# A hybrid attention and retention layer on one core: paired projections traced product by product, retention blocks in thirds, three small operations on other engines

## The chip, the cores and the metric

The kernel runs on one core of one Trainium2 chip. The metric is device microseconds of one execution; the value of a kernel is the median of several runs. The core has TensorE (PE, matmuls and their weight loads), VectorE (DVE), ScalarE (ACT), GpSimd (POOL) and SyncE (SP), each with an instruction queue of its own that is worked off in order. SP and POOL also issue the DMAs of this kernel.

## The reference

One layer for a prompt of 1024 tokens and a sample group of 8 x 4 tokens (1056 columns in all), model width 1024. One input projection `w_in` gives the heads of two branches and three gates; windowed attention and chunkwise retention run side by side, each is projected and they are merged by gates; then `w_o` and a convolutional FFN.

```python
h = rms_norm(x, g_pre_mix) @ w_in
q_a, k_a, v_a, q_r, k_r, v_r, gate_r, gm_a, gm_r = jnp.split(h, split_points(), axis=-1)
o_a = banded_window_attn(q_a, k_a, v_a, pos, sinks)      # window 128, 8 heads, 2 kv heads
...
# retention, 4 heads, chunks of 128, key 128, value 256:
scores = jnp.einsum('bihd,bjhd->bhij', q, k) * dmask[None]
inner = jnp.einsum('bhij,bjhe->bihe', scores, v)
cross = jnp.einsum('bihd,bhde->bihe', q, s0) * q_decay[None, :, :, None]
s_new = jnp.exp(log_g * L)[None, :, None, None] * s0 + jnp.einsum('bjhd,bjhe->bhde', k * k_decay[None, :, :, None], v)
...
y_a = o_a @ w_a_proj
y_r = (jax.nn.silu(gate_r) * o_r) @ w_r_proj
mixed = (jax.nn.sigmoid(gm_a) * y_a + jax.nn.sigmoid(gm_r) * y_r) @ w_o
x = x + rms_norm(mixed, g_post_mix)
x = x + rms_norm(conv_ffn(rms_norm(x, g_pre_ffn)), g_post_ffn)
```

## The kernel before

Every fp32 product is made of three matmuls (`mm3`, lines 256 to 258): each operand is split into a high and a low part (`split`: the high part is an ACT copy, L229, the low part a subtraction, L224 on DVE or L226 on POOL), and high x high, high x low and low x high are summed in PSUM. Besides, the large projections are done with seven products instead of eight (`A11, A12, A22, S1` to `S4`), from sums of weight blocks and of activation columns. One product of the pair stage is 4 x 3 = 12 matmuls of 264 columns.

The stages follow each other: normalisation and the first projections, attention, the attention projection (`w_a`, tile ps_a) with sums of activations on DVE, the **pair stage**, the retention projection (`w_r`, tile ps_m and ps_t; here called the z stage), `w_o`, and the FFN.

*Attention.* `attn_pair` treats two of the four head groups in one block of 128 queries, 16 calls in all: scores, a softmax over them (`comb`, with the sum in `den`), four ACT multiplications by 1/den (L686), four transposes (L689), a split into `ph`, for 14 calls two products `pc` of `ph` with a triangle (L695), and the matmuls with the values (L702), whose two halves are added in `pvt` (L706). The sample group's attention (L745 to L755) follows.

*Pair stage.* Sixteen pairs of 128-column groups of `w_in` are projected, each in two halves of the columns (`in_pair`, a generator that yields after each half): four pairs for q and k of the four retention heads, four for the retention gate, eight for the merge gates. A half uses three PSUM banks q0, q1, q2 (tile ps_q, one buffer each). In the order A11, S1, S2, A12, S3, A22, S4, S2 needs a copy of A11's bank in bank 1 (L876); results leave by ACT copies (L884) or DVE additions (L887). `w_split` makes the high and low parts of the weights, three ahead when a pair begins. Work that follows a half (`post`: rope of q and k by a shuffle and products on DVE and POOL, gates on ACT, stores) is held in PEND until `flush`, after a later S2.

Beside the pairs run the retention of the sample group (`sample(h)`, between whole pairs) and that of the prompt (`head(h)`, eight blocks each). A block takes scores and a transpose of k into a ps_a tile (L1045, L1046), masks and splits them (s, sT), scales k (kt), splits v (vt), multiplies into ps_b, adds q (qs) times the state, updates the state from ps_a (L1066), normalises the output (`finish`, with rs on POOL, L283), transposes it (`turn`, L929) and multiplies it by the gate into z (L1081). PSUM holds three ps_a and two ps_b banks beside the three of ps_q.

*What sets the order.* The program is traced in Python; the framework schedules it on a simulated timeline, so an engine's order follows the traced order only roughly. `BLK` sets how many halves of pairs are traced by each retention block: 20 halves over the 32 blocks. Tile pools hold the buffers: a new tile waits until the buffer that it takes over has been read. Weight loads and gate loads go through SP's queue (`ld`), stores, and the loads of qk and v for the retention, through POOL's (`st`).

*z stage.* When a quarter of the result is complete, `merge` multiplies it by one gate and adds the other branch, two DVE operations of 128x528 (L1155, L1156), 16 times. The z operands are loaded on POOL's queue (L1105) in a fixed order.

Of the kernel before, what the change touches and what calls it, by code (L numbers as in the profile page):

```python
# [18 lines left out]
P = 128  # L19
# [3 lines left out]
NB = 8  # L23
# [82 lines left out]
BLK = 10  # L106
# [15 lines left out]
def trunk(ctx, tc, I, O):  # L122
# [539 lines left out]
    def attn_pair(jp, blk):  # L662
# [22 lines left out]
        for h in range(4):  # L685
            S.mul(comb[:, h, :P], comb[:, h, :P], den[:, h:h + 1])  # L686
# [5 lines left out]
        if blk:  # L692
            pc = AT("pc", (P, 2, 4, P), F32R, bufs=2)
            for s in range(2):
                V.tensor_tensor(out=pc[:, s], in0=f32(ph[:, s]), in1=tri.broadcast_to([P, 4, P]), op=mult)  # L695
# [69 lines left out]
    ps_stack.close()  # L765
    pq = ppool("pq", 1, ps_stack)
    pa = ppool("pa", 3, ps_stack)
# [91 lines left out]
    FILL = [5, 8, 6, 9, 7, 10, 11, 12, 13, 14, 15]  # L859
    NEXT = dict(zip([0, 1, 2, 3, 4] + FILL, [1, 2, 3, 4] + FILL + [None]))  # L860
    PW, PEND = [in_ahead(0)], []

    def in_pair(n):

        ws, post, ops = PW[0], pairs[n][2], {}
        for j in range(2):
            o = TT("pair")
            c11, c12, c21, c22 = (o[:, HW * i:HW * i + HW] for i in range(4))
            bk = [psum(pq, "q%d" % b)[:, :HW] for b in range(3)]
            for p in (A11, S1, S2, A12, S3, A22, S4):  # L870
                t = ops[p] = next(ws) if j == 0 else ops[p]
                ps = bk[{A11: 0, A12: 0, S2: 1, S3: 1, A22: 1, S1: 2, S4: 2}[p]]
                if p == S2:
                    if n == j == 0:
                        TE.matmul(ps, t[:, 0], xop(ex1, p, j, 0)[0], start=True, stop=True)
                    S.copy(out=ps, in_=bk[0])  # L876
                for k in range(4):
                    xh, xl = xop(ex1, p, j, k)
                    mm3(ps, t[:, k], t[:, 4 + k], xh, xl, p in (A11, S1) and k == 0, k == 3,
                        skip_group_check=p not in (A11, S1))  # L880
                if p == S2:
                    flush()
                if p in (A12, S1, S2, A22):
                    S.copy(out={A12: c11, S1: c22, S2: c12, A22: c21}[p], in_=ps)  # L884
                elif p != A11:
                    c = c22 if p == S3 else c12
                    V.tensor_tensor(out=c, in0=ps, in1=c, op=add)  # L887
# [741 lines left out]
```

## Time and profile before

| | us |
|---|---|
| runs | 1716.36, 1713.27, 1716.02; median 1716.02 |
| profiled execution, own time | 1712.92 |
| its span, first to last instruction | 1711.1 |
| start, normalisation | 0 to 50 |
| attention and projections beside it | 50 to 200 |
| end of attention, sample attention | 200 to 252 |
| attention projection | 252 to 299.6 |
| pair stage: sample retention, then the prompt's blocks (first score at 458.6), then pairs alone (from about 700) | 299.6 to 750.6 |
| z stage | 750.6 to 850 |
| `w_o` | 850 to 950 |
| FFN | 950 to 1700 |

How to read it: the windows give, for a stretch of the span, how long each engine was busy and how many instructions it ran. The waits name what released an engine that stood idle. The groups give count and duration for a kind of instruction. A line such as L224 is that of a helper and covers many uses, so the tile's name says which.

### The profile page before, as it was taken

The page shows a single profiled execution, that of the slowest core. Times are in us where ns is not written, and L with a number is a line of the kernel's source. Part 1 is how long each engine was busy: PE and PEld are TensorE (multiplying, and loading weights), DVE is VectorE, ACT ScalarE, POOL GpSimd, SP SyncE. Part 2 cuts the span into 40 slices and gives each one's busy share as a digit, 9 for nine tenths or more (in the row PEclk, how much of TensorE's full clock was granted, in tenths as well). Part 3 has the DMA queues.
Part 4 walks back from the last instruction along what each step waited for, and adds up shares of the span by engine and source line. Part 5 has one row for each costly group of instructions (what it writes and reads, how often), then busy time and mean ns, then how long its engine had stood idle before and what let it go on. Part 6 is the DMA issues. An engine that isn't in the chain of part 4 may idle for free.

```text
span 1711.1 us, 32973 instructions
## 1 busy us (share of the span) xinstructions
PE 1647.4 (96%) x12642; PEld 1600.9 (94%) x12642; DVE 1267.5 (74%) x2283; ACT 891.3 (52%) x2006; POOL 434.6 (25%) x658
## 2 busy tenths in 40 slices
PE   8999989898898999999999999999999999999997
PEld 7999979888887999999878999999999999999997
DVE  7787647799577777557956889888888888445576
ACT  6577634344565665454532555555555556433343
POOL 4211100365344443210111222212212223111101
PEclk9999989999998999999999999999999999999999
DMA  7212313345657776587732244444444447866654
GB/s 195 68 54 64 94 45 114 121 139 164 213 180 230 237 253 198 163 251 219 241 127 74 74 131 146 144 151 151 146 157 151 158 145 239 247 181 199 208 178 152
DMA packets 265871, 273.92 MB, mean 160 GB/s; under 512 B 22784, under 2 KB 225824, under 8 KB 265697
## 3 DMA queue, kind: packets, MB, share of 16 engines
q1 hardware_dynamic: 230673, 151.05, 30.4%
q0 software_dynamic: 35040, 120.77, 20.3%
q8 instruction: 99, 1.62, 0.4%
q14 instruction: 59, 0.48, 0.1%
HBM read 184.24 MB, written 87.49 MB: 159 GB/s over the span
## 4 chain that ended last, share of the span: by engine, by line
PE 59%; DMA 7%; DVE 5%; issue 3%; ACT 1%; POOL 1%; SPq 0%; DVEq 0%; POOLq 0%; ACTq 0%
PE ps_m L258 9%; PE ps_m L256 9%; PE ps_m L257 9%; PE ps_t L257 7%; PE ps_t L256 7%; PE ps_t L258 7%; PE ps_q L256 2%; PE ps_q L257 2%; PE ps_q L258 2%; DMA zt<-in_w_r_proj 1%; DMA w_raw<-in_w_in 1%; DMA zt<-in_w_down 1%; DMA w_raw<-r_d 1%; DMA vt<-v_d 1%; DVE zt L224 1%
## 5 line engine op out<-in xcount | busy, mean ns | idle before, releaser
L224 DVE SCALAR_TENSOR_TENSOR w_lo<-w_raw,w_hi 128x1024 fp32r<-128x1024 f32 x83 | 101.2, 1222 | 70.2 <-ACT w_hi L229 66.4
L256 PE MATMUL ps_t<-xh,w_hi 128*128 128x264 f32 (+2 forms) x524 | 149.2, 285 | 0.0
L257 PE MATMUL ps_t<-xl,w_hi 128*128 128x264 f32 (+2 forms) x524 | 148.7, 284 | 0.0
L256 PE MATMUL ps_m<-xh,w_hi 128*128 128x264 f32 x512 | 146.2, 286 | 2.4 <-ACT Gr L1163 0.9
L258 PE MATMUL ps_t<-xh,w_lo 128*128 128x264 f32 (+2 forms) x524 | 148.0, 283 | 0.0
L258 PE MATMUL ps_m<-xh,w_lo 128*128 128x264 f32 x512 | 145.6, 285 | 1.2 <-DVE w_lo L224 1.2
L257 PE MATMUL ps_m<-xl,w_hi 128*128 128x264 f32 x512 | 145.5, 284 | 0.0
L256 PE MATMUL ps_q<-ex,w 128*128 128x264 f32 x384 | 113.5, 295 | 13.2 <-ACT ps_q L876 8.8
L224 DVE SCALAR_TENSOR_TENSOR w<-w_raw,w 128x512 fp32r<-128x512 f32 x152 | 104.0, 684 | 29.5 <-ACT w L330 28.1
L1379 DVE SCALAR_TENSOR_TENSOR c_out<-u_ext,fconst,c_out 128x1024 f32<-128x1024 f32 x96 | 121.9, 1280 | 2.6 <-ACT c_out L1375 0.4
L229 ACT CAST w_hi<-w_raw 128x1024 fp32r<-128x1024 f32 x62 | 65.2, 1052 | 107.6 <-PE ps_t L257 74.5
L257 PE MATMUL ps_q<-ex,w 128*128 128x264 f32 x384 | 110.8, 289 | 0.0
L258 PE MATMUL ps_q<-ex,w 128*128 128x264 f32 x384 | 110.7, 288 | 0.0
L256 PE MATMUL ps_q<-xh,w 128*128 128x264 f32 x384 | 109.0, 288 | 0.6 <-DVE pair L887 0.6
L257 PE MATMUL ps_q<-xl,w 128*128 128x264 f32 x384 | 109.5, 287 | 0.0
L258 PE MATMUL ps_q<-xh,w 128*128 128x264 f32 x384 | 109.1, 287 | 0.0
L330 ACT CAST w<-w_raw 128x512 fp32r<-128x512 f32 x152 | 94.4, 622 | 27.3 <-PE ps_q L258 23.2
L256 PEld LDWEIGHTS ps_m<-xh,w_hi 128*128 128x128 f32 x512 | 96.3, 188 | 3.3 <-ACT Gr L1163 1.1
L258 PEld LDWEIGHTS ps_t<-xh,w_lo 128*128 128x128 f32 x524 | 98.8, 189 | 0.0
L256 PEld LDWEIGHTS ps_t<-xh,w_hi 128*128 128x128 f32 x524 | 98.6, 188 | 0.1
L257 PEld LDWEIGHTS ps_t<-xl,w_hi 128*128 128x128 f32 x524 | 98.7, 188 | 0.0
L258 PEld LDWEIGHTS ps_m<-xh,w_lo 128*128 128x128 f32 x512 | 96.4, 188 | 1.7 <-DVE w_lo L224 1.6
(465 smaller groups left out, 6264.2 us busy)
## 6 DMA issues: line engine op xcount, KB each, us to landing
w_raw<-in_w_up SPq DMA_DIRECT2D x48, 512.0 KB, 4.5
w_raw<-in_w_in SPq DMA_DIRECT2D x42, 512.0 KB, 5.3
w_raw<-s_d SPq DMA_DIRECT2D x60, 256.0 KB, 3.6
t_d<-t POOLq DMA_DIRECT2D x24, 528.0 KB, 4.0
t<-t_d POOLq DMA_DIRECT2D x24, 528.0 KB, 5.2
t<-in_w_down SPq DMA_DIRECT2D x40, 256.0 KB, 4.8
s_d<-t POOLq DMA_DIRECT2D x20, 512.0 KB, 3.6
w_raw<-in_w_down SPq DMA_DIRECT2D x36, 256.0 KB, 6.7
```

The costliest lines, as they stand in the source:

```text
L224: pinned(V.scalar_tensor_tensor(out=out, in0=in0, scalar=1.0, in1=in1, op0=mult, op1=op))
L229: pinned(S.copy(out=hi, in_=src))
L256: TE.matmul(ps, wh, xh, start=start, stop=False, **kw)
L257: TE.matmul(ps, wh, xl, start=False, stop=False, **kw)
L258: TE.matmul(ps, wl, xh, start=False, stop=stop, **kw)
L330: S.copy(out=t[:, 0:4], in_=src)
L1379: V.scalar_tensor_tensor(out=c[:, NS:], in0=u[:, g, NU + t:NU + t + SEQ], scalar=sc[t], in1=c[:, NS:], op0=mult, op1=add)
```

## The change

It rewrites the pair stage and moves three small kinds of work. In the pair stage:

- The pairs become one stream that yields after each product (`stream`, `adv(n)` takes n products). The order of products is A11, S1, A22 of the half before, S2, A12, S4, S3. A11's bank is copied into bank 1 right after A11. Bank 1 has two buffers, so ps_q uses four PSUM banks, and ps_a two instead of three. The weights of the next pair are split product by product (`in_split`); six are split before the first pair.
- `sample(h)` yields five times, and three products are traced at each yield.
- A retention block is cut in `front` (scores, masks, kt, splits of v and q), `middle` (matmuls with v and the state, the new state, `finish`) and `tail` (transposes, gate, sums). Block g's middle is traced after block g+1's front and before block g-1's tail, with two, one and one products between them: 128 products over the 32 blocks.
- v is loaded one block ahead and has three buffers instead of four; qk loads go to SP's queue; the low part of qs is computed on POOL. The gates of a head are loaded at its blocks 0 and 3.

Elsewhere: in `attn_pair` the four ACT multiplications become one DVE product of 128x4x128, and the `pc` products go from DVE to POOL; in the z stage the merges of m < 4 go from DVE to POOL. The number of matmuls is the same but for one more priming matmul.

```diff
@@ attn_pair
-        for h in range(4):
-            S.mul(comb[:, h, :P], comb[:, h, :P], den[:, h:h + 1])
+        V.tensor_tensor(out=comb[:, :, :P], in0=comb[:, :, :P],
+                        in1=den.rearrange("p (h o) -> p h o", o=1).broadcast_to([P, 4, P]), op=mult)
...
-                V.tensor_tensor(out=pc[:, s], in0=f32(ph[:, s]), in1=tri.broadcast_to([P, 4, P]), op=mult)
+                G.tensor_tensor(out=pc[:, s], in0=f32(ph[:, s]), in1=tri.broadcast_to([P, 4, P]), op=mult)
@@ pair stage
+    pa = ppool("pa", 2, ps_stack)
     pq = ppool("pq", 1, ps_stack)
-    pa = ppool("pa", 3, ps_stack)
     pb = ppool("pb", 2, ps_stack)
...
+    def stream():
+        early = (A11, S1, S2, A12, S4, S3)
...
+        ops = {p: next(ws) for p in early}
...
+                bk = [psum(pq, "q%d" % b)[:, :HW] for b in (0, 2)]
+                b1 = pq.tile([P, 512], F32, name="ps_q1", tag="q1", bufs=2)[:, :HW]
+                bk.insert(1, b1)
...
+                for p in (A11, S1, A22, S2, A12, S4, S3):
+                    if p == A22:
+                        if last is not None:
+                            product(A22, *last)
...
+                        continue
...
+                    product(p, bk[{A11: 0, A12: 0, S2: 1, S3: 1, S1: 2, S4: 2}[p]], ops[p], j, dst)
+                    if p == A11 and nh >= 2:
+                        S.copy(out=bk[1], in_=bk[0])
+                    if p == S4:
+                        V.tensor_tensor(out=c12, in0=bk[2], in1=c12, op=add)
+                    if p == S3:
+                        V.tensor_tensor(out=c22, in0=bk[1], in1=c22, op=add)
+                    if p == S2:
+                        flush()
+                    if j and i + 1 < len(ORDER):
+                        nxt[p] = next(ws)
+                    yield
+                last = bk[1], ops[A22], j, dst
...
-    for h in range(5):
-        run(h)
-        flush()
-        if h:
-            sample(h - 1)
+    adv(18)
+    for h in range(4):
+        for _ in sample(h):
+            adv(3)
...
+            qks[g // 2] = qk2 = ST("qk2", (P, 2, 2 * P), bufs=2)
+            c = NS + P * tt
+            ld.dma_start(out=qk2, in_=qk_d[h].rearrange("i p t -> p i t")[:, :, c:c + 2 * P])
+        vts[g] = ST("vt", (P, 2, 256), F32R, bufs=3)
...
+            qs = ST("qs", (P, 2, P), F32R, bufs=2)
+            split(qs[:, 0], qs[:, 1], q, G)
...
-    for h in range(4):
-        for i, _ in enumerate(head(h)):
-            while done < (8 * h + i + 1) * BLK // 16:
-                next(halves_left)
-                done += 1
...
+    for g in range(NBLK):
+        f, coming = coming, ahead(g + 1)
+        if g % NB in (0, 3):
+            gate(g // NB, g % NB // 3)
+        adv(2)
+        m = middle(g, *f)
+        adv(1)
+        if behind is not None:
+            tail(*behind)
+        adv(1)
+        behind = (g,) + m
...
@@ merge
-        V.tensor_tensor(out=v, in0=v, in1=ga[0], op=mult)
-        V.tensor_tensor(out=v, in0=v, in1=ga[1], op=add)
+        eng = G if m < 4 else V
+        eng.tensor_tensor(out=v, in0=v, in1=ga[0], op=mult)
+        eng.tensor_tensor(out=v, in0=v, in1=ga[1], op=add)
```

Three places in the order of the instructions show what becomes of this. The first is ACT in the pair stage, one half of a pair beside the sample retention. L876 is the copy of bank 0 into bank 1, L884 the evictions, w are weight splits, s0s a split of the sample state. Before:

```order
L884 COPY pair<-ps_q_5051 128x264
L330 CAST w_5155<-s_5149 128x512
L884 COPY pair<-ps_q_4941 128x264
L229 CAST s0s<-s_5209 128x512
L876 COPY ps_q_5050<-ps_q_5049 128x264
L832 ACT_TABLE_LOAD
L832 ACTIVATE pair<-pair 128x1056
L884 COPY pair<-ps_q_5050 128x264
L330 CAST w_5159<-s_5150 128x512
L884 COPY pair<-ps_q_5049 128x264
```

and of the changed kernel, at about the same half, where the copy has L923 and the evictions L902:

```order
L923 COPY ps_q_4981<-ps_q_4979 128x264
L329 CAST w_4997<-w_raw 128x512
L975 ACTIVATE o,ss<-o 32x256
L1007 ACTIVATE t_5031<-ps_a,kdec 128x128
L1009 CAST h_5034<-t_5031 128x256
L902 COPY pair<-ps_q_4980 128x264
L329 CAST w_5054<-s_4995 128x512
L977 ACTIVATE o<-o,rs 32x256
L902 COPY pair<-ps_q_4832 128x264
L831 ACT_TABLE_LOAD
L831 ACTIVATE pair<-pair 128x1056
L902 COPY pair<-ps_q_4981 128x264
```

Before, the copy stood behind the eviction of S1 (5051) and that of the last half's A22 (4941); now it stands ahead of both (4980 and 4832), and A22's bank is another one.

The second place is PE in the pair stage among the retention blocks: the scores and the transpose that begin a block, and pair products around them. Before:

```order
L258 MATMUL ps_q_6368<-xh,w_6081 128x264
L1045 MATMUL ps_a<-qk_6477 128x128
L1046 MATMUL ps_a<-ident,qk_6477 128x128
L929 MATMUL ps_b<-ident,o 128x128 x2
L1045 MATMUL ps_a<-qk_6477 128x128
L1046 MATMUL ps_a<-ident,qk_6477 128x128
L256 MATMUL ps_q_6144<-ex,w_6223 128x264
```

and of the changed kernel:

```order
L257 MATMUL ps_q_6165<-ex,w7x 128x264
L255 MATMUL ps_q_6353<-ex,w_6250 128x264
L1103 MATMUL ps_a<-qk_6310 128x128
L1104 MATMUL ps_a<-ident,qk_6310 128x128
L256 MATMUL ps_q_6353<-ex,w_6250 128x264
```

Before, two blocks of a qk tile begin with only a pair of transposes between them, and the next begins some hundred matmuls later; now one block begins within a product, and the next one 59 rows on. Over the whole stage, the pair matmuls between the beginnings of two blocks were between 0 and 216 and are now, after the first two blocks, between 19 and 60.

The third place is PE at the end of attention: L702 (now L701) are the value matmuls, L745 and L748 (now L744 and L747) the transposes of the sample attention's sc, L753 and L754 its value matmuls, L256 to L258 with ps_a (now L255 to L257) the attention projection. Before:

```order
L702 MATMUL ps_c<-pc,dS_849 128x256 x2
L745 MATMUL ps_b<-ident,sc 128x128 x4
L702 MATMUL ps_c<-ph,vS_141 128x256 x2
L702 MATMUL ps_c<-pc,dS_850 128x256 x2
L745 MATMUL ps_b<-ident,sc 128x128 x4
L753 MATMUL ps_c<-pT,cvt 64x128 x8
L748 MATMUL ps_b<-ident,sc 32x128
L754 MATMUL ps_c<-pT_2268,kv_132 64x128
L753 MATMUL ps_c<-pT,cvt 64x128 x8
L754 MATMUL ps_c<-pT_2268,kv_132 64x128
L256 MATMUL ps_a<-qS_142,w_hi 128x384
```

and of the changed kernel:

```order
L256 MATMUL ps_a<-qS_145,w_hi 128x384
L257 MATMUL ps_a<-qS_144,w_lo 128x384
L701 MATMUL ps_c<-ph,vS_141 128x256 x2
L701 MATMUL ps_c<-pc,dS_850 128x256 x2
L744 MATMUL ps_b<-ident,sc 128x128 x4
L752 MATMUL ps_c<-pT,cvt 64x128 x8
L255 MATMUL ps_a<-qS_874,w_hi 128x384
L256 MATMUL ps_a<-qS_875,w_hi 128x384
L257 MATMUL ps_a<-qS_874,w_lo 128x384
L255 MATMUL ps_a<-qS_876,w_hi 128x384
L256 MATMUL ps_a<-qS_877,w_hi 128x384
L257 MATMUL ps_a<-qS_876,w_lo 128x384
```

Before, the projection began after the last matmul of the sample attention; now 24 of its matmuls lie ahead of that one.

More of the change, by code (lines that the diff above doesn't have):

```diff
@@ L857, in in_ahead @@
         return itertools.chain([next(ws) for _ in range(NPRE)], ws)
[L859 to L881, printed above, removed]
-                    flush()
[L883 to L887, printed above, removed]
-            if j == 1 and NEXT[n] is not None:
-                PW[0] = in_ahead(NEXT[n])
-            PEND.append((post, j, o))
-            yield
@@ L893, in flush, with adv @@
+    STR = stream()
+    def adv(n):
+        for _ in range(n):
+            next(STR, None)
     def flush():
@@ L959, in sample @@
         po = pt[:2 * NS, :256]
+        yield
         TE.matmul(po, h8[:, 0, 0:2 * NS], v8, start=True, stop=False)
@@ L978, in sample @@
             st.dma_start(out=O["ret_sample"][0, bb:bb + 2, h].rearrange("b k e -> k b e"), in_=s0)
+            yield
         os8 = ST("o", (P, 256), bufs=2)[:NS]
```

226 lines of the change are left out of this document (142 added, 84 removed).

## The prediction

> **What bounds the kernel now.** I read the windows by stage first, then the waits of PE inside the stages that lose time, then the operations that the change touches. The profiled execution took 1712.92 us by its own time, 1.8 more than the span that its page begins with:
>
> ```profile
> span 1711.1 us, 32973 instructions
> ```
>
> The stages before the FFN:
>
> ```profile
> 50.00:200.00 150.00, 149.76 (x1144) 148.04 (x1143) 107.51 (x236) 104.78 (x345) 23.03 (x53) 1.00 0.23 67
> 200.00:252.00 52.00, 44.68 (x324) 41.15 (x323) 24.60 (x49) 22.35 (x54) 6.11 (x12) 0.87 0.25 65
> ...
> 299.60:458.60 159.00, 143.94 (x1082) 136.35 (x1081) 131.46 (x226) 69.86 (x168) 76.56 (x73) 0.97 0.49 161
> 458.60:555.00 96.40, 83.00 (x610) 79.23 (x609) 69.07 (x197) 54.63 (x156) 40.08 (x61) 0.91 0.62 198
> 555.00:685.00 130.00, 128.10 (x1053) 126.81 (x1052) 99.94 (x266) 82.26 (x223) 57.20 (x87) 1.00 0.72 229
> 685.00:750.60 65.60, 62.43 (x506) 61.58 (x507) 35.10 (x72) 30.49 (x72) 14.76 (x23) 1.00 0.60 192
> 750.60:850.00 99.40, 92.98 (x714) 89.53 (x714) 75.08 (x122) 51.41 (x87) 5.97 (x8) 1.00 0.76 231
> ```
>
> The columns are the window, its length, then busy time and count of PE, weight loads, DVE, ACT and POOL, the granted PE clock, the DMA share and GB/s. The FFN, from 950 on, is left alone by the change; a stretch of it, below, shows PE full. The pair stage, 299.6 to 750.6, is where PE has holes: its lower granted clock stands in the same two windows as its holes. Busy time alone hides part of the loss, because a matmul beside a wait has a longer record. So I price the work at the rate of the full stretch and take the rest as loss. The first row is that rate (a stretch of the FFN, 264-column matmuls), the four behind it are the pair matmuls (tile ps_q, PE alone) of the four windows.
>
> ```profile
> 1000.00:1050.00 50.00, 50.00 (x414) 50.00 (x413) 44.75 (x77) 27.24 (x60) 14.19 (x24) 1.00 0.45 142
> ```
>
> ```profile
> 299.60:458.60 159.00, 130.99 (x959) 0.97 0.49 161
> 458.60:555.00 96.40, 61.87 (x424) 0.91 0.62 198
> 555.00:685.00 130.00, 108.42 (x829) 1.00 0.72 229
> 685.00:750.60 65.60, 60.22 (x479) 1.00 0.60 192
> ```
>
> 50.00/414 = 0.121 us a pair matmul. The others (123, 186, 224 and 27 by subtraction of the two lists) have 128 or 256 columns; by columns and their mix I estimate 0.1 us each. Work and loss then are: 116 + 12 of 159, **loss 31**; 51 + 19 of 96.4, **loss 27**; 100 + 22 of 130, **loss 8**; 58 + 3 of 65.6, **loss 5**. Together 71 us. The third window is the telling one: retention blocks run there beside pairs, and only 6% is lost. The second has the same blocks and loses 28%.
>
> What PE waits for in the pair stage (us in total, times, longest):
>
> ```profile
> PE ps_q L256 <- ACT ps_q L876: 8.8, 5, 3.1
> PE ps_q L256 <- DVE pair L887: 4.0, 7, 1.0
> PE ps_a L256 <- DVE kt L1053: 3.9, 2, 2.5
> PE ps_q L256 <- ACT pair L884: 3.7, 6, 0.9
> PE ps_b L256 <- ACT sT L229: 2.8, 1, 2.8
> PE ps_b L969 <- DVE s0s L224: 2.4, 4, 1.3
> ```
>
> Two families: the bank copy and evictions of a pair's three ps_q banks (L876, L884, L887: 16.5 us), and links inside one retention or sample step (kt, sT, s0s: 9.1 us), where PE stands at the consumer because the step is issued faster than DVE and ACT can go round it.
>
> **The change, part by part.**
>
> *Pair order and banks.* ps_q gets four banks instead of three. The copy of bank 0 into bank 1 goes out directly after A11, with S1 and the previous half's A22 (24 matmuls, 2.9 us) between it and its first user S2; before, it stood behind the eviction of S1, so only an instant was left. A22's bank is evicted while two other products run. That removes the condition of the 8.8 us at L876 and most of L884 and L887, up to 16.5 us of waits, which the next two terms hold by window. What stays is at the very start, where ACT is held by casts behind a load, which the new order still places ahead of the copies:
>
> ```profile
> ACT v L944 <- DMA vs<-v_d: 5.7, 2, 3.2
> ```
>
> *Retention in thirds.* A block's scores, its middle and its turning into z now lie in three different blocks, with four products (48 matmuls, 5.8 us) handed out two, one and one between them. The pair matmuls between one block's first score and the next were 0 to 216 and are, after the first two blocks, 19 to 60 (36 to 59 from the seventh on). With some eleven small matmuls (1.1 us) a block takes 7 us of PE. DVE's need per block is (69.07 + 99.94 + 35.10)/32 = 6.4 us, less 0.28 for qs below: 6.1, weights included, so DVE fits in at 87%. I give windows two to four (253 us of work by the sums above, loss 40) a loss of 7%, a little over the 6% of the third window, plus 4 for the start and end: 18 + 4 = 22. **Term: -18.** Bounds: -30 (a loss of 4% all through) and +29 (see the second rival).
>
> *Sample parts.* They are traced in fifths with three products after each. DVE has the last word here, not PE:
>
> ```profile
> 340.00:425.00 85.00, 76.49 (x571) 70.98 (x569) 83.42 (x145) 36.34 (x93) 50.18 (x45) 0.98 0.47 149
> ```
>
> 83.4 of 85 us DVE is busy with rope, weights and sample steps, and the change takes nothing from it there. By its share of the stage's length (159 of 451) a third of the 16.5 us of bank waits, 5.8, falls here; with DVE full some of it only moves. **Term: -4**, between -12 and +5.
>
> *Attention.* One step loses four ACT multiplications and gains one DVE multiplication of the same 512 columns; its two pc products go from DVE to POOL. The rows give the count, min/median/max in ns, and where the first and last start; POOL's rows behind them the count, busy time and mean ns, and its idle time before them.
>
> ```profile
> L695 DVE TENSOR_TENSOR pc<-ph,tri x28: 669/683/694, 87.6 to 233.5; 128x512 fp32r<-128x512 f32 x28
> ...
> L686 ACT ACTIVATE comb<-comb,den x64: 386/391/416, 80.8 to 199.7; 128x128 f32<-128x128 f32 x64
> ```
>
> ```profile
> L283 POOL TENSOR_TENSOR rs<-ms,mhalf 128x1 f32<-128x1 f32 x33 | 27.9, 845 | 33.2 <-DVE ms L281 32.9
> L226 POOL TENSOR_TENSOR pair<-pair,rcos 128x528 f32<-128x528 f32 x16 | 25.2, 1574 | 27.7 <-DVE sh L823 27.4
> L226 POOL TENSOR_TENSOR pair<-pair,sh 128x528 f32<-128x528 f32 x16 | 23.5, 1471 | 11.8 <-DVE sh L224 11.7
> ```
>
> ACT loses 64 x 0.391 = 25 us; DVE gains 16 x 0.69 = 11 and loses 28 x 0.683 = 19. POOL has no 128x512 product here; below is DVE's 0.68 us, above the 1.57 of rcos. I take 1.4, nearest to the 1.47 of the slightly larger sh product: 28 x 1.4 = 39 us. Per step the chain changes by 0.69 - 4 x 0.391 = -0.87 and 2 x (1.4 - 0.68) = +1.4, so +0.5 us. From 50 to 200 PE is busy 149.76 of 150 us and covers it. Without cover are the last two or three steps, +1.5 us. But the new order puts the attention projection (ps_a from qS and w) between them. Before, nothing was there (the window, then the wait of PE that is its largest):
>
> ```profile
> 230.00:252.00 22.00, 15.08 (x82) 12.45 (x81) 8.17 (x17) 9.14 (x23) 1.25 (x3) 0.69 0.23 56
> ```
>
> ```profile
> PE ps_c L702 <- DVE pvt L706: 4.8, 3, 4.0
> ```
>
> Of 22 us, 6.9 are empty, and 82 matmuls at 0.1 to 0.12 us would need 10 at most, so 12 are lost; about half can be filled while the projection has work whose inputs exist. -5.5 + 1.5: **term: -4**, between -10 and +3.
>
> *qs low halves to POOL, qk loads to SP.* The operation that moves, the loads that leave POOL's queue, and what ACT waits for there:
>
> ```profile
> L224 DVE SCALAR_TENSOR_TENSOR qs<-qk,qs x28: 279/283/293, 463.3 to 700.3; 128x128 fp32r<-128x128 f32 x28
> ```
>
> ```profile
> L1038 POOL DMA_DIRECT2D qk<-qk_d x16 | 11.9, 742 | 2.0 <-DVE qs L224 2.0
> ```
>
> ```profile
> ACT o L923 <- POOL rs L283: 22.5, 17, 5.0
> ```
>
> DVE gives up 28 x 0.283 = 7.9 us. POOL's price for 128x128 lies between 0.36 (sh's 1.47 us scaled by columns) and the 0.85 of rs, its small operation; 0.5 gives 14 us, against 11.9 us of qk issues that leave its queue. POOL's queue thus stays as full as it was, and rs, for which ACT waits 22.5 us, can come 0.5 us later behind a split. A split is wanted only one block (7 us) later, which covers it. On SP the 16 qk loads now stand behind weight loads that wait for buffers. They are issued about a block ahead, so a wait of SP beyond some 7 us would show as a late front. **Term: 0**, between -3 and +8.
>
> *z stage.* The row is one of the two operations of a merge:
>
> ```profile
> L1156 DVE TENSOR_TENSOR Gr<-Gr,a_in x16: 694/700/834, 774.3 to 856.7; 128x528 f32<-128x528 f32 x16
> ```
>
> Eight of sixteen merges (16 operations of 0.70 us) leave DVE, -11 us, and cost POOL 16 x 1.5 = 24. DVE is busy 75 of 99 us, and PE's 714 matmuls at 0.121 are 86 us, so it loses some 13, of which the relief may return a little. On POOL the last merges stand around a copy that took, as the timeline of POOL has it,
>
> ```profile
> 850.94 5.69 POOL L262 CAST ms<-xh 128x256 fp32r<-128x256 f32 x1 [66.08 <-DVE xl L224]
> ```
>
> so with three operations behind it (3 x 1.5) the last merged half comes near 861 rather than 857. The second half of the columns is read by the projection only after its first token tiles, about 20 us into the stage. **Term: 0**, between -4 and +6.
>
> One rule speaks against the three moves to POOL. Rows first:
>
> ```profile
> L224 DVE SCALAR_TENSOR_TENSOR sh<-sh,rsin x16: 692/802/1837, 311.0 to 418.7; 128x528 f32<-128x528 f32 x16
> ...
> L973 DVE TENSOR_SCALAR kb<-h,bm x32: 265/280/1554, 335.0 to 434.9; 128x128 fp32r<-128x128 f32 x32
> ```
>
> The same DVE operation takes from 0.69 to 1.84 us, the short one up to 1.55, in the stretch where POOL does its rope products. The Trainium skill, "SBUF — State Buffer", section "SBUF: two separate sides", says that DVE and GpSimd share one port pair as an exclusive lock, and that the loser blocks for the whole instruction. The long records agree; the medians, near the minimum, say that most operations escape. By that rule the moved work would hold DVE for up to its POOL time: 75 - 11 + 24 = 88 of 99 us in the z stage, and the sum would be some 5 us less good, 1695; by the medians it stays as worked out.
>
> *Sum.* -18 - 4 - 4 + 0 + 0 = **-26**: 1712.9 - 26 = 1686.9 by the profiled execution. The median of the three runs, 1716.0, is 3.1 above that execution, so **1690** us.
>
> **Rivals.** *The gain mostly moves.* DVE at 83.4 of 85 us says that part of the stage cannot go faster, and POOL's rs (ACT waits 22.5 us) is not relieved. If the retention's chains stay as late as now, only the attention end remains: 1716 - 4 = 1712. For it: no DVE work worth mentioning vanishes. Against: in the third window the same chains cost 6%.
>
> *Slower, by the ps_a banks.* They fall from three to two; the wait that this can multiply occurred once:
>
> ```profile
> PE ps_a L1045 <- DVE state L1066: 0.9, 1, 0.9
> ```
>
> A retention block holds its bank from the scores until the state is read (L1066), and the next block's scores are now issued ahead of that middle, so both banks are in use. If each of the 52 ps_a tiles (four heads, sixteen sample pairs, 32 blocks) met those 0.9 us, that is +47 against -26: 1716 + 21 = 1737. It decides from 26/52 = 0.5 us a tile. Against it: with three banks it was one wait in all, and two products (2.9 us) now lie between front and middle.
>
> *The larger gain.* If the pairs run at the FFN's rate but for the first stalls, the loss of 71 falls to 15: 1716 - 56 - 4 = 1656. For it: every ps_q wait loses its condition. Against: DVE in the sample parts.
>
> *The schedule does not change in effect:* the rows of the order do show the even spacing, so little; 1716.
>
> **Chances.** Forecast (1677 to 1703) 0.50; larger gain 0.17; gain moves 0.17; slower 0.11; no effect 0.05. Over 0.2% means below 1712.6 or above 1719.4, about what a measurement here can tell. Faster: 0.50 + 0.17 + 0.09 = 0.76. Same: 0.07 + 0.05 = 0.12. Slower: 0.11 + 0.01 = 0.12. The range 1660 to 1716 leaves out half of the larger gains (0.08) and the slower cases (0.12).
>
> **What would show it.** Right: L876's successor gone from the PE waits; the pair stage near 429 us long with its clock at 1.00; ps_a waits under 5 us; pc products near 1.4 us on POOL; PE over 18 us busy in the last 22 before the projection. Wrong: many waits of ps_a for state or kt, waits for qk, or DVE full over more than 85 us of the stage.

## The result and the profile after

The changed kernel takes 1688.01 us (median of 4 runs, 1684.05 to 1689.65) against 1716.19 before; the ratio is 0.9829, 95% interval 0.9800 to 0.9858. The forecast was 1690. The profiled execution took 1688.03 us by its own time, 24.9 less than that of before.

The windows of the changed kernel, cut where its stages end (window, length, busy time and count of PE, weight loads, DVE, ACT, POOL, granted clock, DMA share, GB/s):

```profile
50.00:200.00 150.00, 148.91 (x1127) 146.22 (x1126) 118.65 (x238) 88.55 (x286) 49.98 (x74) 1.00 0.24 66
200.00:252.00 52.00, 48.33 (x388) 46.69 (x387) 23.22 (x42) 22.23 (x58) 15.65 (x21) 1.00 0.26 68
230.00:252.00 22.00, 18.33 (x134) 16.69 (x133) 8.00 (x17) 9.23 (x26) 1.81 (x4) 1.00 0.24 63
...
299.60:458.80 159.20, 140.25 (x1080) 135.00 (x1081) 133.65 (x232) 68.77 (x169) 78.05 (x73) 0.98 0.51 162
458.80:555.00 96.20, 92.16 (x752) 90.52 (x751) 74.35 (x195) 60.66 (x171) 41.98 (x69) 1.00 0.74 234
555.00:690.00 135.00, 129.29 (x1057) 127.51 (x1056) 100.07 (x263) 79.99 (x227) 60.13 (x99) 1.00 0.71 225
690.00:729.20 39.20, 38.39 (x313) 37.95 (x313) 21.84 (x42) 20.23 (x43) 8.10 (x13) 1.00 0.68 213
729.20:826.00 96.80, 93.64 (x719) 90.32 (x718) 76.60 (x113) 50.90 (x86) 28.24 (x20) 1.00 0.79 241
```

and the pair matmuls (tile ps_q, PE alone) of the attention projection's stretch and of the four windows of the pair stage:

```profile
252.00:299.60 47.60, 7.47 (x51) 1.00 0.24 91
299.60:458.80 159.20, 130.18 (x960) 0.98 0.51 162
458.80:555.00 96.20, 79.63 (x569) 1.00 0.74 234
555.00:690.00 135.00, 112.13 (x827) 1.00 0.71 225
690.00:729.20 39.20, 36.58 (x289) 1.00 0.68 213
```

Priced as in the prediction (0.121 us a pair matmul, 0.1 for the others) the losses are 31, 9, 12 and 2 us: 54 instead of 71, or instead of 69 where the prediction's sums are not rounded on the way. The pair stage is 429.6 us long instead of 451.0, and 51 pair matmuls (6 us) run before it begins, in time that the end of attention left. Where the 24.9 us came from:

| place | forecast | measured | how |
|---|---|---|---|
| end of attention | -4 | -6 | 51 pair matmuls done before 299.6, 2 before the change |
| sample parts | -4 | 0 | loss 31 and 31 |
| retention blocks and the pairs behind them | -18 | -16 | loss 39 and 23 (40 before by the prediction's rounding) |
| z stage, start to `w_o` | 0 | -3 | 750.8 to 838.1, now 729.2 to 813.3 |

The z stage is taken to end at the first matmul of `w_o`, before and after the change:

```profile
L256 PE MATMUL ps_m<-w_hiT,xh x112: 388/396/632, 838.1 to 943.8; 128*128 128x512 f32 x112
```

```profile
L255 PE MATMUL ps_m<-w_hiT,xh x112: 389/394/499, 813.3 to 918.8; 128*128 128x512 f32 x112
```

By this pricing the sum is -25, as the 24.9 us between the two profiled executions.

In the window from 458 two things went at once. Before, PE stood idle for 13.4 of 96.4 us, and its 83.0 busy us were 13 more than the price of the matmuls in them, at a granted clock of 0.91. Now 4.0 of 96.2 us are idle and 5 are above the price, at a clock of 1.00. So almost half of the gain there came from matmuls whose records became shorter, and a list of waits does not show that half.

The largest waits of PE in the pair stage of the changed kernel (us in total, times, longest):

```profile
PE ps_q L255 <- DVE pair L927: 9.9, 6, 3.0
PE ps_q L255 <- DVE pair L925: 5.1, 5, 1.8
PE ps_a L1103 <- DVE state L1134: 4.3, 4, 1.4
PE ps_a L1030 <- DVE kb L1028: 3.5, 5, 1.2
PE ps_q L255 <- ACT pair L902: 2.6, 3, 1.3
```

The wait for the bank copy (8.8 us) is gone, and so are those for kt and sT. The waits for DVE's additions (L925, L927; L887 before) have grown from 4.0 to 15.0 us: part of the saving was given back at the same banks.

### The profile page after: what moved, and what is told of

Same layout as the page of the kernel before. It is cut to its first block, busy times and chain, and to the rows that moved or that the text cites. A ratio compares the mean times of both kernels' runs of the same rounds, so it can differ in the third digit from the quotient of the medians.

```text
span 1686.2 us, 32968 instructions
## 1 busy us (share of the span) xinstructions
PE 1629.5 (97%) x12643; PEld 1588.5 (94%) x12643; DVE 1269.6 (75%) x2227; ACT 868.4 (51%) x1942; POOL 500.9 (30%) x714
## 4 chain that ended last, share of the span: by engine, by line
PE 68%; DVE 11%; DMA 9%; issue 7%; ACT 3%; POOL 1%; SPq 1%; DVEq 0%; POOLq 0%; ACTq 0%
PE ps_m L255 9%; PE ps_m L257 9%; PE ps_m L256 9%; PE ps_t L256 8%; PE ps_t L255 7%; PE ps_t L257 7%; PE ps_mm L255 3%; PE ps_mm L256 3%; PE ps_mm L257 3%; PE ps_q L255 2%; PE ps_q L257 2%; PE ps_q L256 2%; DMA a_in<-a_d 1%; DVE w L223 1%; DVE w_lo L223 1%
## 5 line engine op out<-in xcount | busy, mean ns | idle before, releaser
L255 PE MATMUL ps_q<-xh,w 128*128 128x264 f32 x512 | 148.6, 291 | 7.5 <-DVE pair L925 5.1
L255 PE MATMUL ps_t<-xh,w_hi 128*128 128x264 f32 (+2 forms) x524 | 148.9, 284 | 0.0
L256 PE MATMUL ps_t<-xl,w_hi 128*128 128x264 f32 (+2 forms) x524 | 148.7, 284 | 0.0
L257 PE MATMUL ps_t<-xh,w_lo 128*128 128x264 f32 (+2 forms) x524 | 148.0, 283 | 0.0
L257 PE MATMUL ps_m<-xh,w_lo 128*128 128x264 f32 x512 | 145.6, 285 | 1.2 <-DVE w_lo L223 1.2
L255 PE MATMUL ps_m<-xh,w_hi 128*128 128x264 f32 x512 | 145.9, 285 | 0.2 <-ACT w_hi L228 0.2
L256 PE MATMUL ps_m<-xl,w_hi 128*128 128x264 f32 x512 | 145.5, 284 | 0.0
L256 PE MATMUL ps_q<-xl,w 128*128 128x264 f32 x512 | 145.4, 284 | 0.0
L257 PE MATMUL ps_q<-xh,w 128*128 128x264 f32 x512 | 145.3, 285 | 0.0
L255 PEld LDWEIGHTS ps_q<-xh,w 128*128 128x128 f32 x512 | 96.3, 188 | 10.0 <-DVE pair L925 7.0
L257 PEld LDWEIGHTS ps_t<-xh,w_lo 128*128 128x128 f32 x524 | 98.7, 188 | 0.0
L256 PEld LDWEIGHTS ps_t<-xl,w_hi 128*128 128x128 f32 x524 | 98.6, 188 | 0.0
L255 PEld LDWEIGHTS ps_t<-xh,w_hi 128*128 128x128 f32 x524 | 98.6, 188 | 0.0
L257 PEld LDWEIGHTS ps_m<-xh,w_lo 128*128 128x128 f32 x512 | 96.3, 188 | 1.7 <-DVE w_lo L223 1.7
L255 PEld LDWEIGHTS ps_m<-xh,w_hi 128*128 128x128 f32 x512 | 96.3, 188 | 0.4 <-ACT w_hi L228 0.4
L256 PEld LDWEIGHTS ps_q<-xl,w 128*128 128x128 f32 x512 | 96.4, 188 | 0.0
L256 PEld LDWEIGHTS ps_m<-xl,w_hi 128*128 128x128 f32 x512 | 96.2, 188 | 0.0
```

The source lines that it names most:

```text
L255: TE.matmul(ps, wh, xh, start=start, stop=False, **kw)
L256: TE.matmul(ps, wh, xl, start=False, stop=False, **kw)
L257: TE.matmul(ps, wl, xh, start=False, stop=stop, **kw)
```

## The experiments

Ratios are to the kernel before, on the chip of the run. The intervals are 0.3 to 0.6% wide, so a part worth less than some 5 us shows in a ratio only at its edge; for such parts the place in the profile is given too. That place comes from one execution each. Up to the z stage e4_merge_back runs the same instructions as the changed kernel in the same order on every engine, and yet its last pair matmul starts at 727.2 us instead of 729.1: differences of some 2 us in this place tell nothing. The rows of the last pair matmul (count, min/median/max in ns, first and last start), the changed kernel and then e4:

```profile
L257 PE MATMUL ps_q<-ex,w7x x128: 278/285/422, 304.3 to 729.1; 128*128 128x264 f32 x128
```

```profile
L257 PE MATMUL ps_q<-ex,w7x x128: 279/285/425, 305.0 to 727.2; 128*128 128x264 f32 x128
```

| run | median us | ratio | 95% interval |
|---|---|---|---|
| changed kernel | 1688.0 | 0.9829 | 0.9800 to 0.9858 |
| e3_unsplit | 1690.3 | 0.9862 | 0.9845 to 0.9878 |
| e2_copy_late | 1690.7 | 0.9874 | 0.9848 to 0.9901 |
| e9_pool_order | 1693.1 | 0.9867 | 0.9841 to 0.9894 |
| e1_attn_back | 1696.6 | 0.9897 | 0.9880 to 0.9914 |
| e10_halves | 1692.1 | 0.9858 | 0.9834 to 0.9882 |
| e8_a22_now | 1694.4 | 0.9868 | 0.9845 to 0.9892 |
| e6_qs_qk_back | 1690.3 | 0.9849 | 0.9820 to 0.9877 |
| e4_merge_back | 1683.5 | 0.9812 | 0.9784 to 0.9839 |
| e11_all_old | 1702.7 | 0.9945 | 0.9925 to 0.9965 |
| e12_before_bank | 1721.7 | 1.0053 | 1.0035 to 1.0070 |
| e13_kb_act | 1682.0 | 0.9831 | 0.9812 to 0.9850 |
| e14_pc_dve | 1686.1 | 0.9832 | 0.9814 to 0.9850 |

### The thirds alone: e3_unsplit

```diff
-        adv(2)
-        m = middle(g, *f)
-        adv(1)
-        if behind is not None:
-            tail(*behind)
-        adv(1)
+        m = middle(g, *f)
+        tail(g, *m)
+        adv(4)
```

with `f = ahead(g)` in place of the front made one block earlier.

> The changed kernel, but each retention block is traced whole (front, middle, tail one behind the other, then four products), with the new product order, the four ps_q banks and the even spacing kept. Theory 1 (the loss of 17.8 us between the first block and 555 us went away because a block's links lie in different blocks): most of it comes back, 1698 to 1706 us, with PE waits for kt, sT or s links of 6 us or more. Rival (the even spacing and the pair banks did it, the thirds add little): 1686 to 1692 us.

1690.3 us; the last pair matmul starts 5 us later (734.3 instead of 729.1). The waits inside a block are back, but small:

```profile
PE ps_b L255 <- ACT sT L228: 3.3, 2, 1.9
```

Theory 1 fell: the thirds alone hold some 5 of the 16 us at most.

### The early copy: e2_copy_late

```diff
                     if p == S2:
...
+                        S.copy(out=bk[1], in_=bk[0])
...
-                    if p == A11 and nh >= 2:
-                        S.copy(out=bk[1], in_=bk[0])
```

> The changed kernel, but the copy of bank 0 into bank 1 is traced at S2 in every half, as before the change; thirds, spacing and four banks kept. My prediction's step (the early copy removes 8.8 us of waits at the copy): waits of ps_q for the copy of 5 us or more return, 1692 to 1698 us. Rival (with A22's bank separate the copy has time enough wherever it is traced, or the scheduler puts it early): 1686 to 1690 us and under 2 us of such waits.

No wait of PE for the copy appears at all, and the last pair matmul is at 728.0, a microsecond earlier than in the changed kernel. The median is 1690.7, and the ratio decides nothing. So where the copy is traced is not what removed those waits. What a copy that runs late would cost, this run does not show: the scheduler put the copies early all the same. Counted by the ACT instructions ahead of them, 18 of the 32 copies stand at the same place as in the changed kernel, 13 one or two places later, one two places earlier.

### The grain: e10_halves

To whole blocks (as in e3) the old grain is added:

```diff
-        adv(4)
+        while done < (g + 1) * 18 // 32:
+            adv(7)
+            done += 1
```

> The changed kernel with whole retention blocks (as in the run with unsplit blocks) and the pairs handed out seven products at a time, about as many per block as before the change: the old grain and the old shape of a block, with the new product order and banks. Theory (the fine grain carries the gain): 1700 to 1708 us, 12 or more above the unsplit run's 1690. Rival (the product order and the fourth bank carry it): 1689 to 1694 us.

1692.1 us, last pair matmul at 732.2. The rival's number: the grain and the thirds, undone together, do not take the gain with them.

### A22 in its own half: e8_a22_now

```diff
-                        if last is not None:
-                            product(A22, *last)
...
-                last = bk[1], ops[A22], j, dst
+                product(A22, bk[1], ops[A22], j, dst)
+                yield
```

> The changed kernel, but A22 is done at the end of its own half, directly behind S3, as the next user of the same bank: thirds, spacing, early copy and four banks kept. My prediction's step (A22 two products later gives DVE and ACT time to read the bank): PE then waits for DVE's addition after S3 in each of the 32 halves, 0.3 to 0.7 us each, 1697 to 1710 us. Rival (the wait is hidden since small retention matmuls stand between): 1687 to 1692 us.

1694.4 us, last pair matmul at 733.7. Between the two: dearer than the rival said, but the waits for DVE's additions are no higher than in the changed kernel (14.0 against 15.0 us), so the cost is not the wait that I named:

```profile
PE ps_q L255 <- DVE pair L923: 7.6, 7, 3.3
PE ps_q L255 <- DVE pair L921: 6.4, 7, 2.2
```

### qs and the qk loads: e6_qs_qk_back

```diff
-            split(qs[:, 0], qs[:, 1], q, G)
+            split(qs[:, 0], qs[:, 1], q)
...
-            ld.dma_start(out=qk2, in_=qk_d[h]...
+            st.dma_start(out=qk2, in_=qk_d[h]...
```

> The changed kernel with the low part of qs on DVE again and the qk loads on POOL's queue again. By the prediction both were worth nothing on the path: 1686 to 1690 us. Rival (DVE is close to its limit beside the blocks, 7.9 us more of it show): 1692 to 1697 us.

1690.3 us, just above the forecast's band; the last pair matmul is 3.5 us later (732.6), and the waits for DVE's additions are 18.5 us instead of 15.0. The move is worth at most a few microseconds.

### All of these together: e11_all_old

The five edits above in one kernel; the fourth bank, the weights ahead, the sample parts, the attention operations and the merges stay as changed.

> The changed kernel with all of these back at once: whole blocks, seven products at a time, A22 at the end of its half, the copy at S2, qs on DVE and qk loads on POOL's queue. Kept are the fourth ps_q bank, weights split product by product for the next pair, the sample parts' five pieces, the attention operations and the merges. Theory now (several conditions each suffice for a part of the same stalls, so each alone costs 0 to 5 us and all together much more than one): 1699 to 1708 us, with the loss between 458 and 555 us back above 20. Rival (what is kept, the bank and the weights ahead, carries the gain): 1690 to 1696 us.

1702.7 us, in the theory's band. The pair stage of this kernel and of the changed one hold the same work, 3196 matmuls, of which 2640 are pairs, from 299.6 to the last pair product:

```profile
299.60:746.60 447.00, 406.08 (x3196) 394.34 (x3197) 332.13 (x758) 230.02 (x610) 184.43 (x241) 0.98 0.61 194
```

```profile
299.60:729.20 429.60, 400.08 (x3196) 390.99 (x3197) 329.90 (x730) 229.65 (x609) 188.26 (x252) 0.99 0.64 203
```

447.0 against 429.6: together they are worth **17.4 us**, all of what the retention and the pairs gained. (The kernel before needs 451.0 for 48 matmuls more, some 6 us, so the fourth bank and the weights ahead, which e11 keeps with the pieces of the sample parts, gain nothing there without the five edits.)

Whether the single costs add up to this is not shown. By the last pair matmul they are 5 or 3 (thirds; thirds and grain), -1 (copy), 5 (A22) and 3.5 us (qs and qk), 11 to 13 in all, each uncertain by some 2 us. By the differences of the ratios from the changed kernel's, times 1714 us, they are 5.0 (thirds and grain), 7.7 (copy), 6.7 (A22) and 3.4 us (qs and qk), 23 in all, against 20 for e11. So the first half of the theory, that each alone is cheap, holds; that together they cost more than their sum does not come out of these runs. One more part of the expectation failed: the loss did not return between 458 and 555 us (11 us by the same prices, 9 in the changed kernel) but later (26 instead of 12 from 555 to 690), with waits spread over many links:

```profile
PE ps_q L255 <- DVE pair L921: 7.2, 6, 3.7
PE ps_q L255 <- DVE pair L919: 5.9, 6, 2.5
PE ps_b L1017 <- ACT s0s L228: 5.5, 4, 2.6
PE ps_b L976 <- ACT o L970: 5.1, 3, 4.1
PE ps_a L1023 <- DVE kb L1021: 4.9, 7, 1.2
```

### The fourth bank alone, in the kernel before: e12_before_bank

```diff
-    pa = ppool("pa", 3, ps_stack)
+    pa = ppool("pa", 2, ps_stack)
...
-            bk = [psum(pq, "q%d" % b)[:, :HW] for b in range(3)]
+            bk = [psum(pq, "q%d" % b)[:, :HW] for b in (0, 2)]
+            bk.insert(1, pq.tile([P, 512], F32, name="ps_q1", tag="q1", bufs=2)[:, :HW])
```

with both halves of the first pair primed.

> The kernel before with one thing of the change: bank 1 of ps_q has two buffers and ps_a two banks instead of three. By my prediction's first step the waits for the copy (8.8 us) go, and part of those for evictions: 1703 to 1709 us on a day when the kernel before takes 1714. By the prediction's slower rival (ps_a waits 0.9 us in each of 52 tiles) it is slower than before, 1725 us or more. Third: no change, 1711 to 1716 us, the waits only move to ps_a.

Slower, 1721.7 us, between the last two numbers: none of the three. The wait for the copy is gone, so the second buffer of bank 1 is enough to remove it, but the time is not won:

```profile
PE ps_q L256 <- DVE pair L888: 11.0, 9, 4.3
PE ps_b L970 <- ACT s0s L229: 8.7, 2, 7.1
PE ps_a L976 <- DVE kb L974: 4.7, 4, 1.9
```

The waits moved to the additions (4.0 us before), to the sample state (0.5 from ACT before) and to ps_a. The attention projection's last matmul starts at 306.6 us instead of 299.5, mostly because pair matmuls now lie among it: up to 306.6 us there are 39 of them here, and 55 in the kernel before, so the delay is some 2 us. The last pair matmul starts 14.6 us later (765.3 instead of 750.7). From the first z matmul to the end of the span it then takes 954.7 us instead of 960.3, although nothing was changed there; why was not tried. Two ps_a banks cost some waits of ps_a here (kb, state, qk), far from 0.9 us in each tile.

### The end of attention: e9_pool_order and e1_attn_back

The projection's matmuls lie among the last attention steps because ps_a's pool is opened first. Back:

```diff
+    pq = ppool("pq", 1, ps_stack)
     pa = ppool("pa", 2, ps_stack)
-    pq = ppool("pq", 1, ps_stack)
```

> The changed kernel with one thing back: the PSUM pool of ps_q is opened before that of ps_a, as before the change, so the attention projection's banks are others. In the order the projection then stands behind the last matmul of the sample attention again. Theory (the 7 us that the end of attention gained come from the projection's banks being free earlier, not from the moved attention operations): 1692 to 1697 us, and PE 15 of 22 us busy between 230 and 252. Rival (the attention operations did it): 1686 to 1690 us.

and the attention operations back, with the pools as changed:

```diff
-        V.tensor_tensor(out=comb[:, :, :P], in0=comb[:, :, :P],
-                        in1=den.rearrange("p (h o) -> p h o", o=1).broadcast_to([P, 4, P]), op=mult)
+        for h in range(4):
+            S.mul(comb[:, h, :P], comb[:, h, :P], den[:, h:h + 1])
...
-                G.tensor_tensor(out=pc[:, s]...
+                V.tensor_tensor(out=pc[:, s]...
```

> The changed kernel with the attention operations back: four ACT multiplications in each step instead of the one on DVE, and the pc products on DVE instead of POOL. Theory (they lie beside a full PE, and at the end the projection fills the gaps either way): 1684 to 1690 us, the window 50 to 200 a little fuller (149.7 of 150 us instead of 148.9). Rival (they made the end of attention shorter): 1692 to 1696 us.

The last matmul of the sample attention (count, min/median/max in ns, first and last start) in the kernel before, the changed kernel, e9 and e1, in this order:

```profile
L754 PE MATMUL ps_c<-pT,kv x4: 273/292/469, 250.0 to 252.8; 128*64 128x128 f32 x4
```

```profile
L753 PE MATMUL ps_c<-pT,kv x4: 272/272/323, 245.4 to 248.1; 128*64 128x128 f32 x4
```

```profile
L753 PE MATMUL ps_c<-pT,kv x4: 273/273/323, 245.2 to 247.9; 128*64 128x128 f32 x4
```

```profile
L753 PE MATMUL ps_c<-pT,kv x4: 273/273/323, 253.5 to 256.2; 128*64 128x128 f32 x4
```

What PE has done by 299.6 us (its busy time and matmuls from the start, for PE alone) in the same order:

```profile
0.00:299.60 299.60, 285.70 (x2019) 0.98 0.31 91
```

```profile
0.00:299.60 299.60, 287.29 (x2068) 1.00 0.31 89
```

```profile
0.00:299.60 299.60, 287.49 (x2060) 0.99 0.31 89
```

```profile
0.00:299.60 299.60, 283.96 (x2014) 0.99 0.30 87
```

The traces speak against both theories. With the projection behind the sample attention again (e9: none of its matmuls ahead of the last one of the sample attention, 24 in the changed kernel) almost nothing is lost: 8 matmuls, 1 us, of the 49 that the change gained; PE is busy 17.38 of 22 us between 230 and 252, not 15, and the last pair matmul starts at 727.4. The times are less clear: the profiled execution took 1684.8 us, the three others 1693, which is in the theory's band, and the ratio leaves it open. With the attention operations back (e1), all of these matmuls are lost again, the sample attention ends 8 us later and the kernel is 1696.6, its interval (0.9880 to 0.9914) apart from the changed kernel's (0.9800 to 0.9858). By the traces the operations carry the gain at the end of attention, and the place of the projection without them brings nothing.

### Which operation: e14_pc_dve

With the merges and kb as in the two runs below, pc is on DVE and the one DVE multiplication stays.

> The run with kb on ACT and the merges on DVE, and in attention the pc products on DVE too: of the attention operations only the one DVE multiplication in place of four on ACT is left. With pc on POOL the DVE operation qS takes 595 ns instead of 283 in its mean, which gives back 10 of the 19 us that DVE lost. Theory (ACT's relief made the end of attention earlier, POOL is not needed): the sample attention ends at 246 to 250 us as in the changed kernel, and the time is 1679 to 1683 us. Rival (DVE's relief by pc was needed): it ends at 252 to 256 us, and the time is 1686 to 1691 us.

```profile
L753 PE MATMUL ps_c<-pT,kv x4: 273/273/323, 250.0 to 252.7; 128*64 128x128 f32 x4
```

The sample attention ends at 252.7, where the rival put it, and the pairs begin 4.6 us later than in e13 (277.6, 273.0). The time is not the rival's when compared by ratio: 0.9832, e13's is 0.9831 (in microseconds, 1686.1, it is at the rival's edge, but the kernel before takes 1715.2 on this chip and 1711.7 on e13's). So pc on POOL brings the end of attention forward by some 4 us, and what that is worth in the whole is below what these runs resolve.

### The merges: e4_merge_back

```diff
-        eng = G if m < 4 else V
+        eng = V
```

> The changed kernel with all merges of the z stage on DVE again. PE lost 3 us less there than before the change. Theory (DVE's relief did that): 1690 to 1692 us and 5 us of loss between the start of z and of w_o, as before the change. Rival (it has nothing to do with the merges): 1686 to 1689 us.

1683.5 us, below both bands: the z stage, from the first z matmul to `w_o`, is as short as in the changed kernel (727.2 to 809.7, 82.5 us; 84.1 there, 87.3 before), so the merges on POOL did not shorten it. The changed kernel's groups in the z stage, 729 to 826 us (busy us, mean ns | idle before):

```profile
L223 DVE SCALAR_TENSOR_TENSOR xl<-Gr,xh 128x264 fp32r<-128x264 f32 x26 | 12.6, 508 | 0.0
L223 DVE SCALAR_TENSOR_TENSOR w_loT<-w_raw,w_hiT 128x1024 fp32r<-128x1024 f32 x7 | 10.4, 1487 | 6.5 <-DMA t<-z_d 4.4 <-ACT w_hiT L246 2.1
...
L1234 POOL TENSOR_TENSOR Gr<-Gr,g_in 128x528 f32<-128x528 f32 x6 | 13.3, 2216 | 54.1 <-ACT g_in L1231 50.5 <-DMA a_in<-a_d 3.6
```

and e4's of the same window:

```profile
L223 DVE SCALAR_TENSOR_TENSOR xl<-Gr,xh 128x264 fp32r<-128x264 f32 x26 | 10.1, 424 | 0.0
L223 DVE SCALAR_TENSOR_TENSOR w_loT<-w_raw,w_hiT 128x1024 fp32r<-128x1024 f32 x7 | 8.5, 1221 | 5.3 <-ACT w_hiT L246 5.3
```

Beside POOL's merges DVE's other operations are longer in their mean, and the first operation of a merge takes 2.2 us there in its mean, not 1.5. DVE's relief was handed back in part. Of the 4.7 us by which e4's span is shorter, 1.9 lie ahead of the z stage, where the two kernels are the same. For the rest there are more runs: from the first z matmul to the end of the span the nine variants of the changed kernel with these merges on POOL take 955.1 to 959.8 us (the changed kernel 957.0), the three with all merges on DVE (e4, e13, e14) 953.0 to 954.3.

### DVE in the sample parts: e13_kb_act

On top of e4:

```diff
-                V.tensor_scalar(out=kb, in0=f32(h8)[:, 1], scalar1=bm[:, bb + b:bb + b + 1],
-                                scalar2=None, op0=mult)
+                S.mul(kb, f32(h8)[:, 1], bm[:, bb + b:bb + b + 1])
```

> The changed kernel with the merges on DVE and, in the sample parts, the 32 products kb on ACT instead of DVE (14 us of DVE time where DVE was busy 83 of 85 us; about 13 us more for ACT, which was busy 36 of 85). Theory (DVE sets the pace of the sample parts): their loss of 23 us falls by 6 to 12, 1672 to 1678 us. Rival (a chain of links sets it, or ACT's queue delays evictions as much): 1681 to 1686 us.

The window of the sample parts in e13 and then in e4:

```profile
340.00:425.00 85.00, 77.94 (x610) 73.88 (x609) 75.35 (x122) 46.66 (x125) 48.51 (x43) 1.00 0.49 153
```

```profile
340.00:425.00 85.00, 76.38 (x590) 73.19 (x588) 82.79 (x145) 37.04 (x95) 49.49 (x43) 0.98 0.49 153
```

DVE fell by 7.4 us and PE did 20 matmuls more in the same 85 us, some 2.4 us; e4 and the changed kernel, with the same order there, differ by 8. The direction is the theory's, the size not: 1682.0 us, ratio as e4's within the intervals. DVE may share in setting the pace there; it does not set it alone. e13 and e4 have the lowest medians, but their intervals overlap the changed kernel's, so none of them is shown to beat it.

## Why the prediction was right

**The sum.** -26 was forecast by the profiled execution, -24.9 came. That it fits so closely is partly luck: by the table the terms were off by -2 (attention), +4 (sample parts), +2 (retention) and -3 us (z stage), and these errors nearly cancel. Of the rivals, the larger gain (1656), the moved gain (1712) and the slower case (1737) did not happen.

**Retention in thirds, -18.** The size was right, -16, and so was the loss (22 forecast, 23 came); the pair stage is 429.6 us long, against 429. The reason was too narrow. I put the gain on spacing and thirds, and the waits of 8.8 us on the place of the copy. The runs show five edits that hold 17.4 us together, the whole of the term, and none of them more than some 5 us by the profile or 8 by the ratio. Whether the same stalls had several conditions, each of them enough, or whether each edit simply adds its own few microseconds, these runs do not decide: their single costs come to 11 to 13 us by one measure and to 23 by the other.

**Pair order and banks.** The waits for the copy went, as said. But e12 takes them away in the kernel before by the second buffer alone and is slower, and in e2 they stay away with the copy traced late. Taking a wait out of the list was not worth its length: after it stood DVE's additions, 4.0 us before and 15.0 now.

**Sample parts, -4.** Came out 0. The step "with DVE full some of it only moves" should have been taken at its word: the window 340 to 425 has DVE at 82.8 of 85 us (83.4 before):

```profile
340.00:425.00 85.00, 74.43 (x582) 70.85 (x580) 82.77 (x143) 36.40 (x94) 48.38 (x43) 1.00 0.49 153
```

**Attention, -4.** -6 came, and PE is busy 18.33 of 22 us from 230 to 252, over 18 as forecast, but the reason was wrong twice, so that the size of this term is luck. I counted the operations at +1.5 us, by the length of one step's chain, and the projection's matmuls at -5.5. The runs show the operations at -8 us of the sample attention's end, and the projection's place at 1 us with them and at nothing without them. Undoing the operations costs 11.7 us by the ratio, twice the -6 of the table; the intervals leave it uncertain by some 6 us, which just allows both. By the end of the sample attention both moves help: from 256.2 (e1) to 252.7 with the multiplication on DVE alone (e14) to 248.1 with pc on POOL too, although pc makes a step's own chain longer. So the length of one step's chain was the wrong measure. The pc products took 1.30 us on POOL (1.4 was taken):

```profile
L694 POOL TENSOR_TENSOR pc<-ph,tri x28: 1279/1301/1533, 85.5 to 226.2; 128x512 fp32r<-128x512 f32 x28
```

**qs and qk, 0.** No wait for qk appears, and the undone move costs at most some 3 us: right within what can be told. The price of the split was a little low: 0.59 us in its median on POOL, where 0.5 was taken.

**z stage, 0.** -3 came, not from the merges; its cause stays open. In e12, whose z stage is that of the kernel before, the stretch up to `w_o` takes 83.6 us, so 87.3 may be what is unusual. The rule that I weighed there fits: the Trainium skill, "SBUF — State Buffer", section "SBUF: two separate sides", has DVE and GpSimd block each other at a shared port pair, and I priced that at 5 us less gain. e4 shows it in DVE's durations (508 against 424 ns, 1487 against 1221). Its median is 4.5 us lower, within the intervals, and the part of this that lies behind the start of the z stage is 2.8 us by the two spans.

**The slower rival.** ps_a's waits grew from 0.9 + 1.2 to 4.3 + 3.5 us (state, kb), more than the 5 us that I gave as the mark, and far below the 26 us from which the case decides.

## What to carry to other kernels

Price a stage by its count of matmuls at the rate of a full stretch: that gave the size of the gain, while the list of waits did not say which edit would bring it. When several edits act on the same stage, undo them one at a time and all at once: here each single trial stayed near the noise, and only the run with all of them back showed what they hold. Take the noise of a place in a profile from two kernels with the same order up to it. Before work is moved from DVE to POOL for relief, look at how long DVE's own operations become beside it.

## What the hardware showed that was not expected

Beside pc on POOL, DVE's split of qS took 595 ns in its mean, up to 1.94 us; with pc on DVE (e1) never above 0.30. The two rows are the changed kernel and e1:

```profile
L223 DVE SCALAR_TENSOR_TENSOR qS<-pvt,qS x32: 276/285/1941, 94.4 to 241.9; 128x128 fp32r<-128x128 f32 x32
```

```profile
L223 DVE SCALAR_TENSOR_TENSOR qS<-pvt,qS x32: 261/284/297, 97.1 to 248.4; 128x128 fp32r<-128x128 f32 x32
```

The median is the same and the maximum seven times as long, so the delay falls on single operations: nine of the 32 take 0.88 to 1.94 us in the changed kernel, and each of the nine overlaps a pc product on POOL; the other 23 stay near the median. In sum it is 10 us (17.9 against 7.9 in the groups), which is more than the 8 us by which the attention operations were to relieve DVE; its busy time between 50 and 200 rose from 107.5 to 118.7 us, and yet the stage's end came earlier.
